# RG-LRU column order, taps read from PSUM, a fifth result place and three order changes in a fused decoder layer

## The chip, the cores and the metric

One core of a Trainium2 chip runs the whole step as one program. The metric is device microseconds of one execution. The engines are TensorE (PE, with its weight loads PEld), VectorE (DVE), ScalarE (ACT), GpSimd (POOL) and the queue engine SP, which only issues transfers.

## What is computed

One layer of a hybrid decoder, for a prompt of 2048 tokens and 8 sample tokens, with D = 1024. The input is normalized and modulated, and one projection `z = hn @ w_in` gives the columns `xa`, `za` (1024 each, for the RG-LRU group) and `q`, `k`, `v`, a low-rank decay and `zg` (for the GLA group). What matters here is the RG-LRU group:

```
xp = concat([conv0, xa], time)                      # 3 old rows in front
xc = conv_b + sum(xp[:, j:j+T] * conv_w[j] for j in range(4))
gx = sigmoid(blockdiag(xc) + b_gate_x);  ga = sigmoid(blockdiag(xc) + b_gate_a)
log_a = 8 * ga * log_sigmoid(lru_lambda);  a = exp(log_a)
h = scan(a, sqrt(1 - a*a) * gx * xc)                # h[t] = a[t] h[t-1] + ...
y_lru = h * silu(za)
```

The GLA group gives `y_gla = rmsnorm(o) * g * silu(zg)`, and both go through `w_out`, a gate, a residual add and a last RMSNorm. The prompt's outputs are compared beside the new states, among them the last three rows of `xa`.

## The kernel before, in words

The prompt is handled in two halves of 1024 tokens (`half` 0 and 1), each in two segments of 512 (`s` 0 and 1). Channels lie on the 128 partitions and tokens along the free axis. All matrix products are fp32 split into a rounded high part and a low rest, three matmuls for one.

The order on TensorE is: a start that loads, normalizes and begins the first GLA head (0 to about 90 us); the GLA heads of half 0 (to 332); the **couples** of half 0 (to 594); the GLA heads of half 1 (to 867); the couples of half 1 (to 1110); and the output projection (to the end).

**Couples** (class `Couple`, `couples()`). A couple is two blocks of 128 columns of the projection, computed for both segments by a Strassen-like scheme of seven products instead of eight. A product is 12 matmuls of 128x512. Products 0 and 3 build up bank `x`, products 2 and 5 bank `zz` (both from the four `acc` banks of PSUM), and 1, 4 and 6 bank `y` (of two `tp` banks). After product 3 the bank `x` holds segment 0 of the first column block; after product 4, line 1597 writes segment 1 of the second block into `x`; after product 5 `zz` holds segment 0 of the second block; after product 6 `y` holds segment 1 of the first. `block(s, n, src)` takes each result. The products of neighbouring couples are interleaved: m2, m3, (m+1)0, m4, m5, (m+1)1, m6, where m2 is product 2 of couple m. Line 1592 writes bank `zz` from `y` after product 2 and must have read `y` before product 4 adds to it.

Two kinds of couples exist. `Zg` holds two blocks of `zg`: each result goes through `silu` on ScalarE into a place `zs`, is multiplied on VectorE (line 1649) with a piece of `o` loaded from DRAM, and is stored. `Lru` holds a block of `xa` and one of `za`. A `za` result goes through `silu` into a place `zs` and waits for the scan. An `xa` result goes into `conv` (lines 1683 to 1706): ScalarE copies it to the tile `xa` behind 3 old columns (L1697) and computes the fourth tap (L1698); VectorE adds the three other taps from the tile `xa` (L1700, three of them), and the result is split into `xh` (ScalarE, L1705) and `xl` (VectorE, L1706). `gates(s)` multiplies `xh` and `xl` on TensorE with two gate matrices (six matmuls, L1718 to L1721) into the two banks `gps` (tags `kv` and `o`), which ScalarE empties by Tanh (L1722). After `gates(1)` come Exp, Sqrt and a Silu of one element named `one` (L1731 to L1733, with a table load each), two products (L1739, L1740) and the scan (L1746) on VectorE, and the results `zs` times the scan (L1757). The tiles `tx`, `tg` and `a` of the gates exist once, so the next couple's Tanh waits for the scan. There are four `zs` places.

**What sets the order.** `after(units, fn)` puts a step off; `tick(0.5)` follows each product, so a unit is two products. `behind(V)` keeps an instruction behind the last one recorded on VectorE. The order on each engine is then made by a planner from estimated durations, the earlier recorded instruction first among those that it holds ready. The first head and the output projection are `in_order`: their order is as written.

**First head** (`gla_head` with `wv`): `vhave(n)` splits the raw value weights of the second head into a high part (ScalarE, L379) and a low part (VectorE, L380), 1.5 and 2.5 units on.

**Output projection** (class `Pair`, lines 2183 and on): for two rows of tokens at once at first, seven products (B11, T2, T1, B21, T3, B22, T4) with weights loaded at its beginning; `split_w` makes their high (L2058) and low parts (L2061), `hi` and `lower` those of the operands S3 and S4, and `sums` (L2217) empties PSUM. `at(g, k, ...)` lists what follows product k of group g.

Of the kernel before, what the change touches and what calls it, by code (L numbers as in the profile page):

```python
# [8 lines left out]
F32 = mybir.dt.float32  # L9
# [44 lines left out]
def hybrid_kernel(ctx, tc, i, o):  # L54
# [1113 lines left out]
    def gla_head(half, h, k, wv=None, w=None):  # L1168
# [34 lines left out]
        if not final:  # L1203
            m = HEADS[k + 1]
            vcols = [(V0 + m * DV, DV, k0, 4) for k0 in (0, 4)]
            vraw = [None, None]

            def vrows(n):
                vraw[n] = ahead(*vcols[n])

            def vhave(n):
                w[n] = take(*vcols[n], vraw[n])

            if half == 0:
                for n in range(2):
                    after((0.5, 0.5)[n] if wv else (1, 1.5)[n], lambda n=n: vrows(n))
                    after((1.5, 2.5)[n] if wv else (2.5, 3.5)[n], lambda n=n: vhave(n))
            else:
                for n in range(2):
                    after((0.5, 2.5)[n], lambda n=n: vhave(n))  # L1220
# [261 lines left out]
    banks, turns = [0], [0, 0, 0, 1]  # L1482
# [5 lines left out]
    class Couple:  # L1488
# [115 lines left out]
        def zs(self):  # L1604
            own = self.more.pop(0) if self.more else None
            if own:
                return own()
            return lp.tile([P, 512], F32, tag="zs", name="zs", bufs=4)
# [3 lines left out]
    class Zg(Couple):  # L1612
# [26 lines left out]
        turn = 0  # L1639
# [5 lines left out]
        def block(self, s, dt, src):  # L1645
            z = self.zs()
            silu(z, src)
            c0 = SEGS[s][0]
            V.tensor_tensor(z, z, self.o[((0, 0), (1, 1), (0, 1), (1, 0)).index((s, dt))], op=OP.mult)
            late_spill(z, 8 + 2 * self.h + dt, self.half, c0)  # L1650
# [3 lines left out]
    class Lru(Couple):  # L1654

        def __init__(self, half, j):
            super().__init__(half, (XA + j * P, ZA + j * P), (16 + j, 8 + j))
# [16 lines left out]
        def block(self, s, n, src):  # L1674
            if n == 1:
                z = self.zs()
                silu(z, src)
                after(2, lambda: self.out(s, z))
            else:
                self.conv(s, src)  # L1680
                after((3.5, 2)[s], lambda: self.gates(s))

        def conv(self, s, src):
            j = self.j
            if s == 0:
                self.cv, self.x2 = [None] * 2, [None] * 2
                self.xa = lp.tile([P, 512 + 4], F32, tag="xa", name="xa")
                if self.half == 0:
                    V.memset(self.xa[:, :3], 0.0)
                else:  # L1690
                    V.tensor_copy(self.xa[:, :3], xac[:, j])
            else:
                V.tensor_copy(self.xa[:, :3], self.xa[:, 512:515])
            xa = self.xa
            cv = self.cv[s] = lp.tile([P, 512], F32, tag=f"cv{s}", name="cv")
            cw = [vecT[:, j, R_CW + k:R_CW + k + 1] for k in range(4)]
            S.copy(xa[:, 3:515], src)  # L1697
            S.activation(cv, src, AF.Identity, scale=cw[3], bias=vecT[:, j, R_CB:R_CB + 1])  # L1698
            for k in range(3):
                V.scalar_tensor_tensor(cv, xa[:, k:k + 512], cw[k], cv, op0=OP.mult, op1=OP.add)  # L1700
            if s == 1:
                V.tensor_copy(xac[:, j] if self.half == 0 else stT[:, j, 0:3], xa[:, 512:515])
# [217 lines left out]
    for k, h in enumerate(HEADS):  # L1920
        w = gla_head(0, h, k, wv0 if k == 0 else None, w)
        if k == 0:
# [10 lines left out]
    zg0.more = [None] * 2 + [lambda: lp.tile([P, 512], F32, tag="cv1", name="zs"),  # L1933
                             lambda: lp.tile([P, 512 + 4], F32, tag="xa", name="zs")[:, :512]]
# [512 lines left out]
    at(0, 1, later(first_two, first_s3), later(first_two, hi, S3), later(first_two, lower, S3), later(load_w, 0, B22, 5))  # L2447
    at(0, 2, later(split_w, 0, T3), later(first_two, first_s4_end), later(load_w, 0, T4, 6))
    at(0, 3, later(first_two, hi, S4), later(split_w, 0, B22), later(first_two, lower, S4), pairs[2].load)
# [98 lines left out]
```

## Time and profile before

| | |
|---|---|
| median of 3 runs | 1442.52 us (1440.55 to 1443.47) |
| profiled execution | 1444.88 us, of which the span from first to last instruction is 1443.1 us |
| mean granted clock of TensorE | 0.993 of full speed |
| busy share of the span | PE 98%, PEld 81%, DVE 74%, ACT 50%, POOL 15% |
| moved by DMA | 341.88 MB, mean 237 GB/s |

In the profile, a line such as L1718 is a line of the kernel before. Times are microseconds from the first instruction. A row of the timeline gives start, duration, engine, line, operation, tiles, shape and count, and in brackets how long the engine was idle before it and what ended that. Matmuls overlap, so their starts tell more than their durations.

### The profile page before, as it was taken

The page shows a single profiled execution, that of the slowest core. Times are in us where ns is not written, and L with a number is a line of the kernel's source. Part 1 is how long each engine was busy: PE and PEld are TensorE (multiplying, and loading weights), DVE is VectorE, ACT ScalarE, POOL GpSimd, SP SyncE. Part 2 cuts the span into 40 slices and gives each one's busy share as a digit, 9 for nine tenths or more (in the row PEclk, how much of TensorE's full clock was granted, in tenths as well). Part 3 has the DMA queues.
Part 4 walks back from the last instruction along what each step waited for, and adds up shares of the span by engine and source line. Part 5 has one row for each costly group of instructions (what it writes and reads, how often), then busy time and mean ns, then how long its engine had stood idle before and what let it go on. Part 6 is the DMA issues. An engine that isn't in the chain of part 4 may idle for free.

```text
span 1443.1 us, 22452 instructions
## 1 busy us (share of the span) xinstructions
PE 1408.6 (98%) x8113; PEld 1166.8 (81%) x8113; DVE 1062.9 (74%) x2335; ACT 725.4 (50%) x1354; POOL 215.6 (15%) x267
## 2 busy tenths in 40 slices
PE   8999999999999999999999999999999999999997
PEld 6888989886877777889898888877888787777886
DVE  5767985657879786766787864787854986597886
ACT  3634454635785878434353433767663622244432
POOL 0200153325232223101112100000012000000000
PEclk9999999999999999999999999999999999999999
DMA  9724755738688476965956529898879777684442
GB/s 320 279 82 158 263 202 199 243 132 288 244 284 297 171 240 238 385 212 172 321 193 233 197 88 319 281 313 282 279 241 407 287 262 237 246 322 149 148 162 102
DMA packets 168899, 341.88 MB, mean 237 GB/s; under 512 B 12466, under 2 KB 96722, under 8 KB 165197
## 3 DMA queue, kind: packets, MB, share of 16 engines
q1 hardware_dynamic: 136981, 275.82, 55.7%
q0 software_dynamic: 14480, 51.26, 9.2%
q10 hardware_dynamic: 17328, 13.37, 2.8%
q8 instruction: 64, 1.05, 0.3%
q14 instruction: 46, 0.38, 0.1%
HBM read 205.78 MB, written 134.69 MB: 236 GB/s over the span
## 4 chain that ended last, share of the span: by engine, by line
PE 61%; DVE 16%; ACT 11%; DMA 6%; issue 4%; POOL 2%; SPq 0%; ACTq 0%; DVEq 0%; POOLq 0%
PE acc L2196 11%; PE tp L2196 8%; PE acc L1582 5%; PE tp L1582 5%; PE acc L707 3%; PE acc L709 3%; PE acc L708 3%; PE acc L402 3%; PE acc L401 3%; PE acc L403 3%; DVE cv L1700 2%; PE po L1070 2%; DVE a L1746 2%; DVE op L1529 2%; DMA wr<-in_w_in_dram 1%
## 5 line engine op out<-in xcount | busy, mean ns | idle before, releaser
L1582 PE MATMUL acc<-op,op 128*128 128x512 f32 x1056 | 252.2, 391 | 0.0
L1582 PEld LDWEIGHTS acc<-op,op 128*128 128x128 f32 x1056 | 197.1, 188 | 42.1 <-issue 0.8
L1582 PE MATMUL tp<-op,op 128*128 128x512 f32 x792 | 192.2, 395 | 3.2 <-DVE acc L1592 2.4
L2196 PE MATMUL acc<-w,a 128*128 128x512 f32 (+1 forms) x792 | 187.5, 389 | 1.5 <-DVE a L2061 1.3
L1582 PEld LDWEIGHTS tp<-op,op 128*128 128x128 f32 x792 | 148.1, 189 | 39.7 <-issue 3.3
L2196 PEld LDWEIGHTS acc<-w,a 128*128 128x128 f32 x792 | 146.5, 188 | 37.8 <-issue 3.4
L401 PE MATMUL acc<-w,op 128*128 128x256 f32 (+1 forms) x508 | 150.7, 297 | 1.3 <-ACT w L379 1.2
L403 PE MATMUL acc<-w,op 128*128 128x256 f32 (+1 forms) x508 | 144.8, 285 | 0.3 <-DVE op L271 0.2
L402 PE MATMUL acc<-w,op 128*128 128x256 f32 (+1 forms) x508 | 144.7, 285 | 0.4 <-DVE w L380 0.4
L2196 PE MATMUL tp<-w,a 128*128 128x512 f32 x564 | 137.5, 393 | 1.2 <-DVE w L2061 1.2
L2196 PEld LDWEIGHTS tp<-w,a 128*128 128x128 f32 x564 | 105.1, 188 | 29.5 <-issue 5.2
L707 PE MATMUL acc<-op,w 128*128 128x512 f32 x296 | 121.1, 409 | 0.0
L709 PE MATMUL acc<-op,w 128*128 128x512 f32 x296 | 116.5, 394 | 0.0
L708 PE MATMUL acc<-op,w 128*128 128x512 f32 x296 | 115.9, 392 | 0.0
L401 PEld LDWEIGHTS acc<-w,op 128*128 128x128 f32 x508 | 96.9, 191 | 2.9 <-ACT w L379 1.6
L402 PEld LDWEIGHTS acc<-w,op 128*128 128x128 f32 x508 | 96.3, 190 | 1.6 <-DVE w L380 0.6
L403 PEld LDWEIGHTS acc<-w,op 128*128 128x128 f32 x508 | 96.3, 190 | 1.1 <-DVE op L271 0.4
L2058 ACT CAST a<-s 128x512 fp32r<-128x512 f32 x61 | 36.5, 620 | 106.4 <-issue 35.4
L228 ACT ACTIVATE junk<-on 128x256 bf16<-128x256 f32 x64 | 26.8, 418 | 120.1 <-DVE on L1075 103.1
L1700 DVE SCALAR_TENSOR_TENSOR cv<-xa,vecT,cv 128x512 f32<-128x512 f32 x96 | 77.0, 802 | 5.1 <-ACT cv L1698 4.2
L717 POOL DMA_DIRECT2D mixd<-zs x37 | 27.8, 754 | 282.7 <-DVE zs L1757 225.6
L1071 DVE TENSOR_TENSOR states<-states,pkv 128x256 f32<-128x256 f32 x60 | 25.0, 417 | 60.8 <-PE po L1070 60.5
(444 smaller groups left out, 2836.8 us busy)
## 6 DMA issues: line engine op xcount, KB each, us to landing
wtd<-op SPq DMA_DIRECT2D x77, 512.0 KB
op<-wtd SPq DMA_DIRECT2D x77, 512.0 KB
w<-parts SPq DMA_DIRECT2D x16, 1024.0 KB
a<-mixd SPq DMA_DIRECT2D x63, 256.0 KB
parts<-w POOLq DMA_DIRECT2D x12, 1024.0 KB, 6.6
w<-wd SPq DMA_DIRECT2D x10, 1024.0 KB
mixd<-zs POOLq DMA_DIRECT2D x37, 256.0 KB, 6.1
wr<-in_w_in_dram SPq DMA_DIRECT2D x18, 512.0 KB
```

The source lines that it names most:

```text
L401: PE.matmul(ps, part(0, kt, c), hi[:, kt % 4], start=kt == 0, stop=False)
L402: PE.matmul(ps, part(0, kt, c), lo[:, kt % 4], start=False, stop=False)
L403: PE.matmul(ps, part(1, kt, c), hi[:, kt % 4], start=False, stop=kt == KT - 1)
L707: PE.matmul(ps[:, :n], hi[:, kt], a, start=kt == 0, stop=False)
L708: PE.matmul(ps[:, :n], hi[:, kt], b, start=False, stop=False)
L709: PE.matmul(ps[:, :n], lo[:, kt], a, start=False, stop=kt == KT - 1)
L1070: PE.matmul(po, qi[:, t], St[h], start=False, stop=True)
L1529: V.tensor_tensor(w[:, 1], x, w[:, 0].bitcast(F32), op=OP.subtract)
L1582: PE.matmul(ps, w[:, u, k], t[:, v, k], start=q < 3 and (k, u, v) == (0, 0, 0), stop=(k, u) == (3, 1), skip_group_check=True)
L1700: V.scalar_tensor_tensor(cv, xa[:, k:k + 512], cw[k], cv, op0=OP.mult, op1=OP.add)
L2058: S.copy(t[:, 0, k], (low(t) if src is None else src)[:, k])
L2196: PE.matmul(ps, t[:, u, k], w[:, v, k, c], start=(q < 3 or ps is own) and (k, u, v) == (0, 0, 0), stop=(k, u) == (3, 1), skip_group_check= ...
```

## The change

The two column blocks of an `Lru` couple change places: `za` is the first and `xa` the second. So `za` comes out after products 3 and 6 and `xa` after 4 (segment 1, kept in its bank) and 5 (segment 0). Both segments' convolutions are recorded after product 5, `gates(0)` 2.5 units and `gates(1)` 3 units later. The tile `xa` and its copy are gone: the taps read the bank itself, shifted by the output's offset, and up to three columns at the left edge get small taps from the saved last three columns. The old tile's place serves as a fifth `zs`, each fifth time. `zg0`, the couple before the last of half 0, loses one extra place, and its third and fourth products with `o` are put off by 1.75 units and recorded `behind(V)`. In the first head the two `vhave` steps come 0.5 units earlier. In the output projection the splits of T3 and B22 each move one step ahead.

```diff
-                    after((1.5, 2.5)[n] if wv else (2.5, 3.5)[n], lambda n=n: vhave(n))
+                    after((1, 2)[n] if wv else (2.5, 3.5)[n], lambda n=n: vhave(n))
...
+            ring[0] += 1
+            if ring[0] % 5 == 0:
+                return lp.tile([P, 512 + 4], F32, tag="xa", name="zs")[:, :512]
             return lp.tile([P, 512], F32, tag="zs", name="zs", bufs=4)
...
+            def late():
+                with behind(V):
+                    mult()
+            if self.wait_o and s != dt:
+                after(self.wait_o, late)
+            else:
+                mult()
...
-            super().__init__(half, (XA + j * P, ZA + j * P), (16 + j, 8 + j))
+            super().__init__(half, (ZA + j * P, XA + j * P), (8 + j, 16 + j))
...
         def block(self, s, n, src):
-            if n == 1:
+            if n == 0:
                 z = self.zs()
                 silu(z, src)
                 after(2, lambda: self.out(s, z))
+            elif s == 1:
+                self.second = src
             else:
-                self.conv(s, src)
-                after((3.5, 2)[s], lambda: self.gates(s))
+                self.cv, self.x2 = [None] * 2, [None] * 2
+                self.conv(0, src)
+                self.conv(1, self.second)
+                after(2.5, lambda: self.gates(0))
+                after(3, lambda: self.gates(1))
...
-            if s == 0:
-                self.cv, self.x2 = [None] * 2, [None] * 2
-                self.xa = lp.tile([P, 512 + 4], F32, tag="xa", name="xa")
-                if self.half == 0:
-                    V.memset(self.xa[:, :3], 0.0)
-                else:
-                    V.tensor_copy(self.xa[:, :3], xac[:, j])
-            else:
-                V.tensor_copy(self.xa[:, :3], self.xa[:, 512:515])
-            xa = self.xa
...
-            S.copy(xa[:, 3:515], src)
             S.activation(cv, src, AF.Identity, scale=cw[3], bias=vecT[:, j, R_CB:R_CB + 1])
             for k in range(3):
-                V.scalar_tensor_tensor(cv, xa[:, k:k + 512], cw[k], cv, op0=OP.mult, op1=OP.add)
-            if s == 1:
-                V.tensor_copy(xac[:, j] if self.half == 0 else stT[:, j, 0:3], xa[:, 512:515])
+                n = 3 - k
+                V.scalar_tensor_tensor(cv[:, n:], src[:, :512 - n], cw[k], cv[:, n:], op0=OP.mult, op1=OP.add)
+                if s or self.half:
+                    V.scalar_tensor_tensor(cv[:, :n], xac[:, j, k:], cw[k], cv[:, :n], op0=OP.mult, op1=OP.add)
+            V.tensor_copy(stT[:, j, 0:3] if s and self.half else xac[:, j], src[:, 509:512])
...
-    zg0.more = [None] * 2 + [lambda: lp.tile([P, 512], F32, tag="cv1", name="zs"),
-                             lambda: lp.tile([P, 512 + 4], F32, tag="xa", name="zs")[:, :512]]
+    zg0.more = [None] * 2 + [lambda: lp.tile([P, 512], F32, tag="cv1", name="zs")]
+    zg0.wait_o = 1.75
...
-    at(0, 1, later(first_two, first_s3), later(first_two, hi, S3), later(first_two, lower, S3), later(load_w, 0, B22, 5))
-    at(0, 2, later(split_w, 0, T3), later(first_two, first_s4_end), later(load_w, 0, T4, 6))
-    at(0, 3, later(first_two, hi, S4), later(split_w, 0, B22), later(first_two, lower, S4), pairs[2].load)
+    at(0, 1, later(first_two, first_s3), later(first_two, hi, S3), later(first_two, lower, S3), later(split_w, 0, T3),
+       later(load_w, 0, B22, 5))
+    at(0, 2, later(first_two, first_s4_end), later(split_w, 0, B22), later(load_w, 0, T4, 6))
+    at(0, 3, later(first_two, hi, S4), later(first_two, lower, S4), pairs[2].load)
```

## Rows read from the trace of the kernel before

**Rows 1.** The page's busy time, share of the span and instructions of each engine

```profile
PE 1408.6 (98%) x8113; PEld 1166.8 (81%) x8113; DVE 1062.9 (74%) x2335; ACT 725.4 (50%) x1354; POOL 215.6 (15%) x267
```

**Rows 2.** TensorE's waits by line: released by, total us, times, longest us

```profile
PE gps L1718 <- ACT xh L1705: 4.4, 5, 1.5
PE tp L1582 <- DVE acc L1592: 2.4, 1, 2.4
...
PE pkv L1064 <- DVE kTl L1046: 1.7, 1, 1.7
...
PE acc L2196 <- DVE a L2061: 1.3, 1, 1.3
PE acc L401 <- ACT w L379: 1.2, 1, 1.2
PE tp L2196 <- DVE w L2061: 1.2, 1, 1.2
```

**Rows 3.** Stretches: length, busy time by engine, then granted clock, DMA share, GB/s

```profile
459.08:482.70 23.62, 23.62 (x117) 18.82 (x116) 17.06 (x22) 20.26 (x31) 5.83 (x4) 1.00 0.54 216
529.95:555.02 25.07, 24.27 (x117) 18.58 (x116) 21.41 (x30) 19.86 (x32) 6.79 (x5) 1.00 0.72 242
583.65:587.06 3.41, 3.33 (x8) 2.66 (x9) 3.38 (x5) 0.00 (x0) 0.01 (x1) 0.50 1.03 359
```

**Rows 4.** Timeline of TensorE from gates(0) to gates(1) of an early couple

```profile
367.30 0.62 PE L1721 MATMUL gps<-xl,amh 128*128 128x512 f32 x2
367.76 5.61 PE L1582 MATMUL acc<-op,op 128*128 128x512 f32 x24
373.21 0.40 PE L1718 MATMUL gps<-xh,amh 128*128 128x512 f32 x1
```

**Rows 5.** Timeline of PE, ACT and DVE around the seventh Lru couple of half 0

```profile
526.73 0.51 PE L311 MATMUL gps<-sel,am 128*128 128x8 f32 x4
...
526.94 0.20 ACT L1733 ACTIVATE one<-a 128x1 f32<-128x1 f32 x1
...
531.08 2.28 DVE L1746 TENSOR_TENSOR_SCAN a<-tg,tx 128x1024 f32<-128x1024 f32 x1
...
537.22 0.62 ACT L1705 CAST xh<-cv 128x512 fp32r<-128x512 f32 x1 [0.42 <-DVE cv L1700]
...
552.14 0.20 ACT L1733 ACTIVATE one<-a 128x1 f32<-128x1 f32 x1
```

**Rows 6.** VectorE's groups by line and shape: count, busy us, mean ns, idle before

```profile
L1700 DVE SCALAR_TENSOR_TENSOR cv<-xa,vecT,cv 128x512 f32<-128x512 f32 x96 | 77.0, 802 | 5.1 <-ACT cv L1698 4.2
...
L1289 DVE SCALAR_TENSOR_TENSOR xb<-acc,xb 128x512 f32<-128x512 f32 x7 | 4.8, 689 | 3.9 <-PE acc L709 3.9
...
L1702 DVE COPY xac<-xa 128x3 f32<-128x3 f32 x8 | 1.3, 163 | 1.6 <-ACT xa L1697 1.6
```

**Rows 7.** Timeline: last matmul of gates(0), and the Tanh emptying its second bank

```profile
370.04 0.68 ACT L1722 ACTIVATE tg<-gps,hba 128x512 f32<-128x512 f32 x1
...
530.99 0.63 PE L1721 MATMUL gps<-xl,amh 128*128 128x512 f32 x2
...
536.12 0.69 ACT L1722 ACTIVATE tg<-gps,hba 128x512 f32<-128x512 f32 x1 [1.98 <-DVE cv L1700]
```

**Rows 8.** Timeline of VectorE at the end of half 0's couples

```profile
577.70 1.22 DVE L1739 SCALAR_TENSOR_TENSOR a<-tg,a 128x1024 f32<-128x1024 f32 x1 [3.81 <-ACT one L1733]
...
582.98 0.69 DVE L1592 TENSOR_TENSOR acc<-tp,p 128x512 f32<-128x512 f32 x1
```

**Rows 9.** Timeline of ScalarE at the end of the first head

```profile
84.88 0.64 ACT L972 ACTIVATE e<-e 128x512 f32<-128x512 f32 x1
...
90.74 1.98 ACT L379 CAST w<-wr 128x1024 fp32r<-128x1024 f32 x2
```

**Rows 10.** Timeline of VectorE early in the output projection

```profile
1138.06 2.50 DVE L2061 TENSOR_TENSOR w<-w 128x512 fp32r<-128x512 f32 x4 [0.61 <-ACT w L2058]
1140.48 1.29 DVE L2061 TENSOR_TENSOR a<-s,a 128x512 fp32r<-128x512 f32 x2
```

More of the change, by code (lines that the diff above doesn't have):

```diff
@@ L1480, in open_s @@
         lp.tile([P, 1], F32, tag="one", name="place")
-    banks, turns = [0], [0, 0, 0, 1]
+    banks, turns, ring = [0], [0, 0, 0, 1], [0]
     def gps():
@@ L1637, in product @@
             super().product(q)
-        turn = 0
+        turn = wait_o = 0
         def load_o(self, n):
@@ L1648, in block, with mult @@
             c0 = SEGS[s][0]
-            V.tensor_tensor(z, z, self.o[((0, 0), (1, 1), (0, 1), (1, 0)).index((s, dt))], op=OP.mult)
-            late_spill(z, 8 + 2 * self.h + dt, self.half, c0)
+            x = self.o[((0, 0), (1, 1), (0, 1), (1, 0)).index((s, dt))]
+            def mult():
+                V.tensor_tensor(z, z, x, op=OP.mult)
+                late_spill(z, 8 + 2 * self.h + dt, self.half, c0)
+            def late():
[5 more added lines that the diff above has]
+                mult()
     smp_lru = {}
```

## The prediction, as written before the result was known

> **What bounds the kernel now.** I read the busy times first: TensorE is busy for 1408.6 us of a span of 1443.1, and the next engine, VectorE, for 1062.9 [rows 1]. The change takes no matmul away, so what it can win is TensorE's 34.5 us of idle time and what that idle time costs in clock. The second view is therefore TensorE's list of waits [rows 2]. Six of its rows are places that the change touches or lies beside: 4.4 us before `gates` (five times, released by the cast `xh`), 2.4 us once before a product of a couple (released by L1592 on VectorE), 1.7 us in a GLA chunk, 1.3 and 1.2 us early in the output projection, 1.2 us at the first product of the second head. The third view is the clock in stretches [rows 3]: in 583.65 to 587.06, which begins as the 2.4 us wait ends, the granted clock is 0.50, that is the level of 1.2 GHz instead of 2.4. TensorE was full before that wait. So this wait cost 2.4 us and half of 3.41 us more, 1.7, together 4.1.
>
> Next, why `xh` is late. An undisturbed couple takes 23.62 us and has no idle TensorE; the seventh `Lru` couple of half 0 takes 25.07, with 24.27 busy [rows 3]. Around it, `one` runs at 526.94 and again at 552.14 [rows 5]: ScalarE and VectorE need 25.2 us for a round that TensorE does in 23.6. The round is visible: `one` ends the chain of table loads, VectorE may then run L1739 and so on to the scan at 531.08, the taps of segment 1 come among and behind these, `xh` ends at 537.84, then come the gates, their Tanh, and the next chain to `one`. Product 6 ended just before the small matmuls at 526.73 [rows 5], so this convolution took 11.1 us, where TensorE has only three products and one set of gates to do in between. A product is 2.72 us (5.45 for two, from start to start) and a gate matmul 0.23, six of them 1.4 [rows 4]: 9.6 us with what is left of the small matmuls some 10.0. It does not fit, and the gates wait.
>
> **The convolutions and gates.** `xa` now leaves the couple after products 4 and 5, and both convolutions are recorded after product 5. From there to `gates(1)` TensorE has five products, one set of gates and in half 0 the small sample matmuls: 5 x 2.72 + 1.4 = 15.0 us, and 16.4 in half 0 (a 23.62 us couple has 1.8 beyond seven products, 19.0, and two sets of gates, 2.8; I take 1.4 of it for the sample matmuls, an estimate). In that time there must now be two convolutions. The worst old one, 11.1 us, plus three more taps of 0.69, three small ones of 0.16 (the three-column copy, the nearest row) makes 13.7 [rows 5, 6]. The margin is 2.7 us in half 0 where it was below zero. In half 1, by the same sum with the longest wait of 1.5 [rows 2] added to 9.6 and 2.6 to 3.1 more for two convolutions, 14.2 stands against 15.0: little, but not late. `gates(0)` come a product and their own 1.4 us ahead of that, 12.3 us behind product 5 in half 0, with one convolution to wait for. I take 4.0 of the 4.4 us as won; the ends are 0 (convolutions start later than recorded, since ScalarE is in its table chain) and 4.4.
>
> The round itself also gets shorter, by this sum: after `one`, L1739 and L1740 (1.2 each, L1739 in [rows 8]), six taps with their small ones (about 5), `xh` 0.6, gates 1.4, then Tanh and the chain as before, about 8.5: some 18 to 19 us. The path over the scan (2.3 behind the taps, then the next Tanh, which writes the tiles that the scan reads) comes to 21 or 22. Both are below 23.6, so lateness should not grow from couple to couple. These are estimates from the rows' durations; the order is the planner's.
>
> What the edit does to the engines: ScalarE loses 32 copies, VectorE loses 48 tiny instructions and gets 32 copies and 72 small taps (three at each `conv` but the first segment of half 0): 56 more at 0.16, 9 us. The taps themselves go from 802 ns with both inputs in SBUF to the 689 ns of the same operation with one input in a bank [rows 6]: 96 x 0.113 = 10.8 us less. So VectorE's load stays as it is; all of it lies beside TensorE. Bound: if a tap from a bank is no faster, 9 us more over 16 couples, 0.6 each, out of a margin of 2.7.
>
> The Trainium skill speaks against this edit: VectorE: DVE Perf Modes, section Rules for kernel authors, says to copy out of PSUM first if many operations follow, and its section on the TRN2 errata gives an instruction that reads PSUM 62 cycles of 0.96 GHz more, 65 ns. By it the taps would take 6.2 us more instead of 10.8 less, 0.4 us per couple's six, an estimate from that page; the row of L1289 against that of L1700 says the opposite.
>
> Banks: bank `x` now stays taken until the taps of segment 1 are done. Of the four `acc` banks three are in use when (m+2)0 takes one, so it is not what TensorE waits for. The silu of product 3 must be done before L1597 overwrites `x`; it is recorded ahead of the gates' Tanh and has two products' time. The fifth `zs` place covers the result that now comes earlier and lives longer: without it a fifth would be needed at product 3. I cost these at nothing; if the cover fails, a silu waits for a store, and a couple is late by a microsecond or two.
>
> **The end of half 0.** The 2.4 us wait is for L1592 at 582.98, on a VectorE that had stood idle for 3.81 us until `one` let L1739 start at 577.70 [rows 8]; three products with `o` and two splits then stood ahead. The change moves two of those (0.6 each) behind L1592, and with the gates no longer late `one` comes at least 1.6 us earlier (the two waits of half 0, 0.8 each, inside the 4.4). 1.2 + 1.6 is more than 2.4. What is put off has only its store, on POOL's queue, behind it, and no product of TensorE. I take all of it, 4.1 with the clock; ends 0 and 4.1.
>
> **The first head.** The split L379 ran at 90.74 behind the Exps of the decay; recorded one step earlier it can follow L972, which ends at 85.52 [rows 9]. The low part is 1.2 us of VectorE put into a chain that then delivers everything else 1.2 later, and the second half's low part may become the late one. The store of the split weights, which POOL issues half a unit behind, comes earlier with it, on a queue with nothing else to do there. Of the 1.2 us [rows 2] I take 0.8; ends -0.6 and 1.2.
>
> **The output projection.** T3's low parts come before two `sums`, so its wait (1.2) goes. But the next one, for the low part of S4 at 1140.48 [rows 10], stands behind the same VectorE work in another order: it can come earlier only by the idle 0.61 at 1138.06, which came from ScalarE doing S4 before B22. TensorE gets there earlier and waits longer. Net 0.6 of 2.5; ends 0 and 2.5. SP's order does not change; ScalarE asks for B22's weights about 4 us earlier, and if they have not landed by then the split waits for them, which is the end at 0.
>
> **Sum.** 4.0 + 4.1 + 0.8 + 0.6 = 9.5 us. The profiled execution took 1444.88 us, 1.78 more than its span, and lies 2.4 above the median of 1442.52. It would come to 1435.4, the median to 1433.0.
>
> **The rivals.**
> *A new wait on the `gps` banks (slower).* Between `gates(0)` and `gates(1)` there is now one product, 2.72 us, instead of two, and both need the same two banks. In the seventh couple the last matmul of `gates(0)` ended at 531.62 and the second bank was empty at 536.81, 5.2 us later [rows 7], 2.0 beyond a product and the two matmuls (0.47) before that bank is needed; in the early couple it was 367.92 to 370.72, 2.8, covered [rows 4, 7]. The taps now queue ahead of the scan for which the Tanh waits, which makes it worse. 16 couples at half of 2.0 up to all of it lose 16 to 32 us; at 17, 1442.5 - 9.5 + 17 = 1450. It decides from 0.6 us a couple. Against it: the order is free on TensorE, so the next product can go ahead, and `gates(0)` come 2.72 us later themselves, by which most of the 5.2 has passed. Chance 0.15.
> *The convolutions start no earlier.* ScalarE is in its table chain when product 5 ends, and the fourth tap comes behind `one`; the gates wait as before. Then 5.5 us remain: 1437. For it: `one` at 526.94 is about when product 6 ended. Chance 0.18.
> *Nothing in sum.* The planner makes a new order everywhere behind the first edit, and waits of 1 to 2 us, some with 1.7 us of slow clock, come up elsewhere: 1440 to 1445. Chance 0.12.
>
> **Chances and range.** Forecast 1433, its own range 1428 to 1437, 0.55. Below lie cases where the 1.7 us in the GLA chunk [rows 2] happens to go too. Two parts in a thousand, 2.9 us, is what a measurement here tells from no change: faster than 1439.6 is the forecast and most of the second rival, 0.71; same 0.14; slower 0.15. The range for 8 in 10 is 1427 to 1444.
>
> **What would show it.** TensorE's wait for `xh` gone from its list, couples 23.6 us apart through half 0, no clock of 0.50 near 580, L1700 near 0.69. T3's wait gone and the S4 wait near 1.8. Wrong: rows in which PE waits at L1718 for ACT's Tanh, or a new wait above 1.5 us with a drop of the clock behind it.

## The result: slower by 0.85 %, and the profile after

The changed kernel takes 1455.22 us (median of 6 runs, 1453.47 to 1457.58) against 1442.08 (6 runs, 1440.55 to 1444.74): a ratio of 1.0085, 95 % interval 1.0071 to 1.0098. The forecast was 1433.0, the range ended at 1444. Its profiled execution took 1455.03 us with a span of 1453.2, 10.1 more than the span before. The busy times of the page, then TensorE's list of waits (released by, total us, times, longest us):

```profile
PE 1412.1 (97%) x8113; PEld 1166.2 (80%) x8113; DVE 1059.4 (73%) x2391; ACT 709.2 (49%) x1322; POOL 219.8 (15%) x267
```

```profile
PE acc L401 <- DMA w<-parts: 3.8, 1, 3.8
PE gps L311 <- ACT am L305: 3.6, 4, 1.1
PE gps L1729 <- ACT xh L1716: 3.3, 2, 2.4
PE gps L1729 <- ACT tx L1733: 2.7, 7, 0.7
PE gps L304 <- DMA raw<-in_w_in_dram: 2.2, 3, 0.8
...
PE tp L2207 <- DMA w<-wd: 1.9, 1, 1.9
PE acc L2207 <- DVE a L2072: 1.8, 1, 1.8
```

Beside [rows 2]: the waits for `xh` (L1716, before L1705) are fewer but not gone, the wait of 2.4 us for L1592 shrank to two of 0.3, and the two of 1.2 us are gone. New are the waits for Tanh (`tx`) and for two loads of weights (`parts`, `wd`); those for `am` and for the load `raw` were 0.4 and 0.3 us before. In the couples of half 0 TensorE waits for `am` (3.6), `raw` (2.2) and Tanh (1.2) and no longer for `xh`; in those of half 1 for `xh` (3.3) and Tanh (1.4). Behind the waits for `parts` and `wd` the clock fell, which the stretches show (length, busy times, then granted clock, DMA share, GB/s):

```profile
597.03:600.44 3.41, 3.41 (x17) 3.41 (x16) 1.63 (x2) 2.48 (x3) 1.06 (x2) 0.50 1.02 420
1126.10:1129.51 3.41, 3.41 (x10) 2.64 (x9) 1.46 (x3) 0.62 (x1) 0.00 (x0) 0.50 1.04 412
```

Each begins 0.8 and 1.0 us after TensorE's wait (3.84 and 1.86 us) had ended, and in it the granted clock is 0.50, that is 1.2 GHz. With half of 3.41 us the first of them costs 5.5 us, the second 3.6.

The lengths of the stages in us, from TensorE's timeline. The first ends at the second head's first product. The couples are counted from the start of their first matmul to the start of their last one, so the wait of 3.84 us for half 1's first weights, and the slow clock behind it, stand in the row of the GLA heads of half 1. "RG-LRU alone" is an experiment below.

| stage | before | after | RG-LRU alone |
|---|---|---|---|
| start | 91.8 | 89.6 | 91.5 |
| GLA heads, half 0 | 240.7 | 238.9 | 237.6 |
| couples, half 0 | 260.9 | 263.5 | 263.5 |
| GLA heads, half 1 | 273.9 | 278.4 | 276.9 |
| couples, half 1 | 242.1 | 246.8 | 245.8 |
| output projection and end | 333.8 | 336.0 | 336.6 |

The couples of half 0 lost most of the wait at the end of the stage (4.1 us expected there) and still got 2.6 longer, those of half 1 4.7. What happened in them is to be seen on ScalarE. Its timeline in the kernel before has the fourth tap (L1698), the first of the chain of three table loads, the copy `am`, and segment 1's copy and fourth tap:

```profile
513.70 0.78 ACT L1698 ACTIVATE cv<-acc,vecT 128x512 f32<-128x512 f32 x1
...
520.47 1.28 ACT L1731 ACT_TABLE_LOAD   x1
...
525.28 0.35 ACT L305 COPY am<-gps 128x256 f32<-128x256 f32 x1
...
529.03 0.60 ACT L1697 COPY xa<-tp 128x512 f32<-128x512 f32 x1
529.51 0.80 ACT L1698 ACTIVATE cv<-tp,vecT 128x512 f32<-128x512 f32 x1
```

Segment 0's convolution began 6.8 us ahead of the chain of Exp, Sqrt and Silu, segment 1's behind it (`one` at 526.94, [rows 5]). The same place in the changed kernel: TensorE's product 5 (it ends at 518.60), VectorE's L1597, which puts product 4's result into its bank (until 520.13), then ScalarE:

```profile
515.72 2.88 PE L1582 MATMUL acc<-op,op 128*128 128x512 f32 x12
```

```profile
519.44 0.69 DVE L1597 TENSOR_TENSOR acc<-tp,p 128x512 f32<-128x512 f32 x1
```

```profile
518.47 1.28 ACT L1742 ACT_TABLE_LOAD   x1
519.77 1.24 ACT L1742 ACTIVATE tg<-tg,lc 128x1024 f32<-128x1024 f32 x1
521.01 1.28 ACT L1743 ACT_TABLE_LOAD   x1
522.31 1.06 ACT L1743 ACTIVATE a<-a 128x1024 f32<-128x1024 f32 x1
523.28 0.76 ACT L1707 ACTIVATE cv<-acc,vecT 128x512 f32<-128x512 f32 x1
524.05 1.28 ACT L1744 ACT_TABLE_LOAD   x1
525.35 0.20 ACT L1744 ACTIVATE one<-a 128x1 f32<-128x1 f32 x1
525.46 0.76 ACT L1707 ACTIVATE cv<-acc,vecT 128x512 f32<-128x512 f32 x1
...
526.63 0.37 ACT L305 COPY am<-gps 128x256 f32<-128x256 f32 x1
...
535.60 0.62 ACT L1716 CAST xh<-cv 128x512 fp32r<-128x512 f32 x1 [1.73 <-DVE cv L1712]
...
552.39 0.20 ACT L1744 ACTIVATE one<-a 128x1 f32<-128x1 f32 x1
```

Both convolutions now fall into the chain. They begin at 523.28, 4.7 us after product 5, and the last cast ends at 536.22. The copy `am`, for which TensorE waits at L311, ran between Sqrt and the last table load before (525.28); now the Identities stand there, and it comes behind them. From `one` to `one` it is 27.0 us, where it was 25.2 [rows 5]. VectorE in the same stretch:

```profile
524.07 1.53 DVE L1710 SCALAR_TENSOR_TENSOR cv<-acc,vecT,cv 128x509 f32<-128x509 f32 x2 [3.94 <-ACT cv L1707]
...
530.59 0.74 DVE L1710 SCALAR_TENSOR_TENSOR cv<-acc,vecT,cv 128x510 f32<-128x510 f32 x1
...
532.13 2.28 DVE L1757 TENSOR_TENSOR_SCAN a<-tg,tx 128x1024 f32<-128x1024 f32 x1
```

It idles 3.94 us for the first tap, and then taps stand ahead of the scan, which runs 6.8 us behind `one` (4.1 before [rows 5]). In most couples the scan is recorded at the end of the next couple's product 5, as before; new is that this couple's convolutions are recorded in that product, ahead of it. Over the whole kernel VectorE stood still for the Identity 39.2 us, where it was 4.2 [rows 6]; the row of its list of waits:

```profile
DVE cv L1710 <- ACT cv L1707: 39.2, 14, 5.1
```

In half 1 it goes further; in one round `one` and the scan are 14.2 us apart:

```profile
967.02 0.20 ACT L1744 ACTIVATE one<-a 128x1 f32<-128x1 f32 x1
```

```profile
981.17 2.34 DVE L1757 TENSOR_TENSOR_SCAN a<-tg,hc,tx 128x1024 f32<-128x1024 f32 x1
```

### The profile page after: what moved, and what is told of

Same layout as the page of the kernel before. It is cut to its first block, busy times and chain, and to the rows that moved or that the text cites. A ratio compares the mean times of both kernels' runs of the same rounds, so it can differ in the third digit from the quotient of the medians.

```text
span 1453.2 us, 22466 instructions
## 1 busy us (share of the span) xinstructions
PE 1412.1 (97%) x8113; PEld 1166.2 (80%) x8113; DVE 1059.4 (73%) x2391; ACT 709.2 (49%) x1322; POOL 219.8 (15%) x267
## 4 chain that ended last, share of the span: by engine, by line
PE 60%; DVE 17%; ACT 8%; DMA 7%; issue 5%; POOL 3%; SPq 1%; ACTq 0%; DVEq 0%; POOLq 0%
PE acc L2207 11%; PE tp L2207 8%; PE acc L1582 6%; PE tp L1582 4%; PE acc L401 4%; PE acc L402 4%; PE acc L403 4%; PE acc L707 3%; PE acc L709 3%; PE acc L708 3%; DVE cv L1710 3%; DVE a L1757 2%; PE po L1070 2%; DMA wtd<-op 1%; DVE op L1529 1%
## 5 line engine op out<-in xcount | busy, mean ns | idle before, releaser
L401 PE MATMUL acc<-w,op 128*128 128x256 f32 (+1 forms) x508 | 151.0, 297 | 3.9 <-DMA w<-parts 3.8
L401 PEld LDWEIGHTS acc<-w,op 128*128 128x128 f32 x508 | 97.1, 191 | 5.5 <-issue 4.2
L1710 DVE SCALAR_TENSOR_TENSOR cv<-acc,vecT,cv 128x510 f32<-128x510 f32 (+2 forms) x96 | 71.0, 742 | 40.0 <-ACT cv L1707 39.2
```

What stands on the lines that cost most here:

```text
L401: PE.matmul(ps, part(0, kt, c), hi[:, kt % 4], start=kt == 0, stop=False)
L1710: V.scalar_tensor_tensor(cv[:, n:], src[:, :512 - n], cw[k], cv[:, n:], op0=OP.mult, op1=OP.add)
```

## The experiments

All were timed in turns with the kernel before; the number in brackets is the 95 % interval of the ratio, and runs of different experiments are best compared by these ratios. Several expectations count in products what the edit gives in units of `after`. A unit is two products, and the product in which a step is put off already counts as its first half unit. So the three experiments on the time of the gates move them by one product; "half a product later" moves the convolutions to the end of product 5, ahead of the next product; and the first segment's convolution that is put off by one unit is recorded one product later, ahead of product 4, and not "with the sixth product".

**The parts alone.** The kernel before with one part of the change: the RG-LRU part (columns, convolutions, gates, bank taps, fifth place), the late multiplications of `zg`, the first head's earlier `vhave`, the output projection's order. Then the last three together. Edits as in the diff above.

> The kernel before with the RG-LRU part alone (columns exchanged, both convolutions recorded with the sixth product, taps from the projection's banks, fifth place). Theory T (the two convolutions together make ScalarE's and VectorE's round longer than TensorE's 23.6 us, and the lateness is passed on to the DMA queue that starts half 1 and the output projection): the whole loss is here, 1456 to 1461 us, the stages of couples 2 to 5 us longer each, VectorE's scan 4.6 us or more behind ScalarE's Silu load. Rival A (the couples lose only what their own stages show, the rest of the loss comes from the gate columns' late multiplications and the small order changes): 1446 to 1450 us. Rival B (the convolutions are harmless): 1438 to 1442 us.

> The kernel before with the gate columns' late multiplication (1.75 products) alone. Theory T: the 2.4 us stall at 582.98 and the dip of the clock at 583.65 go and nothing takes their place, 1437 to 1439 us. Rival A: half 1's first weights come late as in the changed kernel (3.8 us at 596.2 and a dip of the clock there), 1441 to 1446 us.

> The kernel before with the first head's value rows half a product earlier alone. Theory T: 0.8 us less, 1440.5 to 1442 us. Rival (it also takes away the stall near 225 us and its dip of the clock, which the changed kernel no longer has): 1438.5 to 1440 us.

> The kernel before with the output projection's new order alone. Theory T: 0.6 us less, 1441 to 1442 us; the changed kernel's 2.5 us longer output projection comes from the couples being late, not from this order. Rival A: the new order itself costs there, 1443 to 1445 us.

> The kernel before with the three small parts (first head, late multiplications of the gate columns, output projection) and without the RG-LRU part. All theories: the three ratios measured alone (0.9992, 0.9995, 0.9993) multiply to 0.998, 1439 to 1441 us. If a transfer that sets the start of half 1 or of the output projection takes over: 1442 us.

RG-LRU alone: 1454.2, 1.0070 [1.0047, 1.0093]. `zg` alone: 0.9992 [0.9979, 1.0006]; first head: 0.9995 [0.9982, 1.0009]; output projection: 0.9993 [0.9982, 1.0004]; the three together 0.9992 [0.9978, 1.0005]. So nearly the whole loss is in the RG-LRU part (2 us below theory T's range, the stages longer as T said), and the other three win nothing that can be measured, alone or together. With `zg` alone TensorE's waits show where part of its 4 us went:

```profile
PE acc L898 <- DMA wr<-in_w_in_dram: 1.6, 2, 1.0
...
PE tp L1582 <- DVE acc L1592: 1.2, 1, 1.2
...
PE acc L401 <- DMA w<-parts: 0.9, 1, 0.9
```

The wait for L1592 fell from 2.4 to 1.2; then TensorE came earlier to half 1's first weights and waited for them, and for `wr`.

**Scan ahead of the taps, first try.** The first tap of each convolution pinned behind the last recorded scan.

```diff
+                with tc.issue_after(tail[0]) if tail[0] is not None and k == 0 else ExitStack():
+                    V.scalar_tensor_tensor(cv[:, n:], src[:, :512 - n], cw[k], cv[:, n:], ...)
```

> The changed kernel, but VectorE's first tap of each convolution is pinned behind the scan of the block before, so that the scan runs first again. Theory T (the taps that stand ahead of the scan make the round long): the scan comes again about 4 us behind the small Silu instead of up to 14, the waits on Tanh (1.6 and 2.5 us) and most of the late stores and loads go, 1448 to 1452 us. Rival B (what hurts is that both convolutions now come late and together; putting the scan ahead only makes the casts xh later, and the gates wait for them instead): 1455 to 1462 us, Tanh waits exchanged for longer waits on xh.

1453.0, 1.0068 [1.0053, 1.0083]. It changed nothing: in all rounds but one the scan still ran 4.6 to 13.5 us behind `one`, because a block's scan is recorded after the next block's convolutions, so the pin caught the scan of one block earlier. It decides nothing about T.

**Convolutions recorded at the end of product 5**, and so behind the scan of the couple before, in both halves, and then in half 0 alone.

```diff
-                self.conv(0, src)
-                self.conv(1, self.second)
+                def convs():
+                    self.conv(0, src)
+                    self.conv(1, self.second)
+                after(0.5, convs)
```

> The changed kernel, with both convolutions recorded half a product later, behind the copy of the sampled columns' sums. Rival C (ScalarE's order: the two Identity instructions of the convolutions stand ahead of the copy am, and TensorE waits for that copy, 4.3 us in the couples of half 0): those waits fall to the 0.6 us of before, 1450 to 1453 us. Theory T: the copy comes earlier, but the casts xh come later by as much, 1454 to 1458 us.

> The changed kernel with both convolutions recorded half a unit (one product) later in half 0 alone, where that gave couples of 259 us against 263.5, and as changed in half 1. Theory B with the lateness passed on to half 1's first weights: couples of half 0 at 259 us and the stall on these weights under 1 us instead of 3.8, with its dip of the clock gone: 1446 to 1449 us. Rival (the first weights of half 1 are late by themselves): 1450 to 1453 us.

Both halves: 1459.9, 1.0115 [1.0098, 1.0132]; rival C's waits went, its time didn't come, and it is 2 us above T's range too. The scan is back at 3.8 us behind `one` in most rounds of half 0, the waits for `am` are nearly gone and half 0's couples take 259.2 us; but half 1's take 259.3 against 246.8, and the gates wait for `xh`:

```profile
PE gps L1731 <- ACT xh L1718: 12.3, 9, 2.5
```

Half 0 alone: 1450.5, 1.0059 [1.0045, 1.0072], couples of half 0 at 259.6: the rival's range. The couples came out as expected, the stall on half 1's weights did not: still 2.7 us. So in half 0 the taps ahead of the scan do cost some 4 us (for T), and putting them behind it costs more in half 1 (for B).

**Second segment earlier.** Identity and wide taps of segment 1 recorded with product 4.

```diff
             elif s == 1:
                 self.second = src
+                self.taps(1, src)
```

> The changed kernel, but the second segment's Identity and its three wide taps are recorded with the fifth product, where that segment arrives; only its three narrow taps wait for the first segment. Rival B (both convolutions at once are the cause): most of the waits on xh, am and Tanh go, 1446 to 1450 us. Theory T (taps ahead of the scan): there are as many of them ahead of the scan, the scan is no earlier, 1453 to 1457 us.

1464.5, 1.0138 [1.0122, 1.0154]: against both theories. ScalarE's timeline says why recording earlier didn't mean running earlier:

```profile
527.03 1.06 ACT L1750 ACTIVATE a<-a 128x1024 f32<-128x1024 f32 x1
528.00 0.76 ACT L1708 ACTIVATE cv<-acc,vecT 128x512 f32<-128x512 f32 x1
528.78 1.28 ACT L1751 ACT_TABLE_LOAD   x1
```

The result of product 4 also falls into the chain: L1597 has it in its bank at 524.88, the chain runs from 523.20 to 530.27. So its convolution still starts between Sqrt and Silu. And the small taps and `xac` now hold up the bank: 2.5 us of new waits of products for `xac`.

**Gates wider apart**: `after(2.5, ...gates(0))` to `after(2, ...)`. This gives `gates(0)` the place among the products that they had in the kernel before.

> The changed kernel with the first segment's gates 2 products behind the convolutions instead of 2.5, so that the two sets of gates are a whole product apart, not half. Rival D (gates too close together, so that the second set waits for the banks until Tanh has read them: 1.6 and 2.5 us): these waits go, 1450 to 1452 us. Theories T and B: TensorE then waits for xh instead, 1454 to 1459 us.

1462.9, 1.0137 [1.0120, 1.0153]. Rival D falls: Tanh waits are left (1.6 us in four, 2.7 before this edit), and `xh` costs up to 5.6 us at once. That `gates(0)` come a product later in the changed kernel is not what made it slow.

**Scan ahead of the taps, second try.** The scan recorded with the second gates, and the taps pinned behind it.

```diff
-            after(0.5, self.scan)
+            self.scan()
```

> The changed kernel with the scan recorded together with the second gates (a product before the next block's convolutions, where it was recorded after them) and the first tap of each convolution pinned behind it: VectorE now has scan, output products, then taps. Theory T (taps ahead of the scan are the cause): the scan comes some 4 us behind the small Silu everywhere, 1447 to 1451 us. Rival B (from the sixth product on there is too little time for both convolutions beside the scan: whichever of the two is second is late): the Tanh waits go, the waits of the gates on xh grow as they did when the convolutions were recorded a step later (4.5 and 9.6 us), 1455 to 1462 us.

1492.8, 1.0337 [1.0308, 1.0365]. Now the scan does run 3.1 to 3.7 us behind `one` in nearly every round, and the kernel is 36 us slower than the changed one by the two ratios. T falls as the main cause: with the scan first the kernel is far slower. VectorE stands still at the head of its queue until `one` is there (first row, of its own list of waits), and what TensorE needs of it comes late (second row, TensorE's list):

```profile
DVE a L1752 <- ACT one L1746: 53.1, 15, 8.1
```

```profile
PE tp L1582 <- DVE acc L1592: 17.3, 9, 4.8
```

**Taps from SBUF in the changed kernel**: the old body of `conv` with the copy to `xa`; columns, time and gates as changed. The tile `xa` takes its place back, so the fifth `zs` place is gone as well.

```diff
-                V.scalar_tensor_tensor(cv[:, n:], src[:, :512 - n], cw[k], cv[:, n:], ...)
+                V.scalar_tensor_tensor(cv, xa[:, k:k + 512], cw[k], cv, ...)
```

> The changed kernel, but with the tile xa and its copy again: the taps read SBUF as before, and columns, times and order are the changed ones. Rival E (taps from the bank are the cause: they hold the banks): 1444 to 1449 us. Theories T and B (the bank is harmless, the time of the convolutions is the cause): as slow as the changed kernel or slower by the two copies of 0.57 us in each round, 1455 to 1462 us.

1468.6, 1.0158 [1.0122, 1.0194], some 10 us slower than the changed kernel by the ratios, and above the ranges of all three theories. E gets no support, and in the changed kernel's list no product waits for a tap. What the copies cost and what the lost fifth place costs, this run doesn't tell apart.

**Only the second segment from the bank**, columns and times as before, with the three small parts; then the same in half 1 alone.

```diff
+            if s:
+                self.bank_taps(src)
+                return
```

> The kernel before with the three small parts, and in the RG-LRU columns only the second segment's taps read from the projection's bank (that segment's copy and the shift of three columns go; columns, times and the first segment stay as before). Theory B: the convolutions stay apart, each round saves a copy of 0.57 us on ScalarE, and VectorE's taps get 0.06 us shorter: the waits of the gates on xh fall, 1437 to 1440 us. Rival E (taps from a bank hold it and TensorE waits for the bank): 1443 to 1450 us, with new waits of the products on a bank.

> The kernel before with the three small parts, and in half 1 alone the second segment's taps from the projection's bank (in half 0 that kernel's couples took 261.9 us against 257.1, in half 1 240.4 against 241.5). Theory B: 1439 to 1441 us, the first version that would beat both. Rival (differences of a microsecond in the couples are taken back by the transfers that follow): 1441 to 1443 us, no different from the kernel before.

In both halves 1445.5, 1.0005 [0.9994, 1.0016]: neither B's gain (the waits for `xh` stay at 4.2 us) nor E's waits for a bank. In half 0 one wait of 2.4 us for `am` came up. In half 1 alone 1439.5, 0.9983 [0.9973, 0.9992].

**First segment's convolution put off by one unit in the kernel before**, from a copy made after product 3. It is recorded after the next couple's product 0, ahead of product 4.

```diff
             S.copy(self.xa[:, 3:515], src)
+            if s == 0:
+                after(1, lambda: self.taps(0, self.xa[:, 3:515]))
+            else:
+                self.taps(1, src)
```

> The kernel before, in which only the first segment's convolution is put off: its block is still copied to xa after the fourth product, but its Identity, taps and casts are recorded two products later, with the sixth product, as in the changed kernel. Columns, gates, banks and the second segment's convolution stay. Theory B (the convolution of the first segment was worth its place two products earlier; put beside the second one it makes ScalarE's and VectorE's round late): slower, 1452 to 1468 us, with waits on am, Tanh or xh as in the changed kernel and rounds of 26 us or more from one small Silu to the next. Rival F (it is the exchange of the columns, through z and the order of the output products, not the time of the convolution): 1441 to 1446 us, waits as before.

1438.7, 0.9969 [0.9957, 0.9981]: faster, and outside both ranges. It does not decide on B, since the convolution is not beside the second one, as B's price supposes. The rows of ScalarE:

```profile
510.82 0.57 ACT L1694 COPY xa<-acc 128x512 f32<-128x512 f32 x1
...
513.08 0.82 ACT L1704 ACTIVATE cv<-xa,vecT 128x512 f32<-128x512 f32 x1
...
516.91 1.28 ACT L1737 ACT_TABLE_LOAD   x1
```

Put off, it still starts ahead of the table chain, by 3.8 us, from data that lies ready in SBUF. TensorE's waits for `xh` fell with it to 1.1 us in the whole kernel, in two, where they were 4.4 [rows 2]; both are in half 1.

**The recorded time of the gates.** Second gates (and what hangs on them) a product earlier in the changed kernel, a product later in the kernel before.

```diff
-                after(3, lambda: self.gates(1))
+                after(2.5, lambda: self.gates(1))
```

```diff
-                after((3.5, 2)[s], lambda: self.gates(s))
+                after((3.5, 2.5)[s], lambda: self.gates(s))
```

> The changed kernel with the second gates recorded one product (0.5 unit) earlier, together with the first ones, as in the kernel before; what hangs on them (Exp, Sqrt, scan) is recorded a product earlier too, so that the scan stands again before the next block's convolutions. Theory G (the product by which the second gates and the scan were put off is the cause): 1440 to 1448 us, the scan 4 us behind the small Silu. Theory H (the blocks of xa come later: segment 0's with the sixth product instead of the fourth, so that its convolution and casts cannot be done by the time of the gates): still 1452 to 1464 us, with the waits of the gates on xh grown.

> The kernel before with the second gates, and so Exp, Sqrt and scan, recorded one product (0.5 unit) later, nothing else. Theory G: 1450 to 1460 us, the scan 4.6 us or more behind the small Silu and Tanh waits. Theory H: 1440 to 1446 us.

Earlier in the changed kernel: 1478.8, 1.0262 [1.0241, 1.0284], although the scan is back at 3.3 to 3.8 us in most rounds. TensorE then waits for Tanh and `xh`:

```profile
PE gps L1729 <- ACT tx L1733: 10.1, 7, 2.0
PE gps L1729 <- ACT xh L1716: 8.9, 3, 6.1
```

Later in the kernel before: 1446.6, 1.0031 [1.0019, 1.0044], with the scan 3.0 to 4.9 us behind `one`, not later than before, against G. So second gates a product later cost about 4 us there. G falls by the first run; H has the sign of both, but the first is 15 us beyond its range and the second 0.6 us. G also supposes a difference that the two kernels don't have: `gates(1)` are recorded after product 0 of the couple after the next in both (2 units from product 6 before, 3 units from product 5 now), and the scan with them. These two runs tell what it costs to move the second gates, not what the change moved.

**The gains together**: the three small parts, the first convolution put off, and in half 1 segment 1 from the bank.

> The kernel before with what gained or at least did not lose so far: the first segment's convolution put off by two products from a copy that is made at once (0.997 alone), the three small parts, and in half 1 the second segment's taps from the bank (0.998 together). Theory H (what the convolutions need is time between the arrival of their data and the gates; here the first has 15 us and its data is there from the fourth product, the second as before): no new waits, 1434 to 1438 us, faster than both kernels. Rival: both gains are the same waits on xh in half 1, taken away twice, 1438 to 1440 us, no better than the better of the two.

1439.7, 0.9982 [0.9971, 0.9993]: faster than both kernels, but not better than the first convolution put off alone: the rival's range, not H's. The couples of half 0 fell to 255.8 us, the shortest of all, and half 1's weights took it back, with a stretch of slow clock that began in this wait and went on behind it (589.50 to 593.00 at 0.50):

```profile
PE acc L401 <- DMA w<-parts: 3.9, 1, 3.9
```

## Why the prediction was wrong, step by step

**The step that failed** is the sum of the convolutions: 13.7 us of work, set against the time from the end of product 5 to `gates(1)` ("The margin is 2.7 us in half 0", and 14.2 against 15.0 in half 1). It lets both convolutions start when the product ends. In the couple shown ScalarE had gone into its table chain at 518.47, product 5 ended at 518.60, and product 4's result was in its bank at 520.13. The first Identity came at 523.28, 4.7 us after product 5, and the last cast ended at 536.22, 17.6 us after it instead of 13.7 and past the 16.4 that were counted. From the first Identity on it took 12.9 us. (The 13.7 already hold one late start: the old convolution of 11.1 us, from which they were made, began at 529.03, 2.3 us after product 6.)

What this cost is not what the sum looked at. In half 0 no gates waited for `xh` any more, where it had been 0.8 us twice. TensorE had been held up by other things first:

```profile
519.34 1.07 PE L304 MATMUL gps<-raw,fs 128*32 128x256 f32 x16 [0.74 <-DMA raw<-in_w_in_dram]
...
527.05 0.61 PE L311 MATMUL gps<-sel,am 128*128 128x8 f32 x4 [0.96 <-ACT am L305]
...
538.03 0.50 PE L1729 MATMUL gps<-xh,amh 128*128 128x512 f32 x1 [0.67 <-ACT tx L1733]
```

In half 1, where the margin was 0.8, two waits for `xh` are left, 0.95 and 2.38 us, where three had made 2.8. So of the 4.4 us only 1.1 were won, and the waits that the prediction put at nothing grew by 7.8: `am` from 0.4 to 3.6, Tanh from none to 2.7, `raw` from 0.3 to 2.2. For `am` the rows show the reason, the Identities ahead of it on ScalarE. The load `raw` was asked for at 512.36, where it had been 506.07; what held it back is not shown.

The prediction had the late start as a rival (chance 0.18, "ScalarE is in its table chain when product 5 ends, and the fourth tap comes behind `one`") and gave it 1437, as if it only forfeited the 4.0 us. That price was the second error. The kernel before had one convolution ahead of the chain and one behind it; the changed one has both in it.

How far this is shown: that nearly the whole loss lies in the RG-LRU part is measured (1.0070 of 1.0085). That both convolutions begin inside the chain, and what TensorE then waits for, are rows. That the start inside the chain is the cause is argued. Seven runs kept the exchanged columns and moved a step or the scan; the best is 1.0059, and none got both convolutions ahead of the chain in most couples. Nearest to a test come the two that record the convolutions at the end of product 5: in half 0 they then begin behind `one` and let `am` and the scan go first, and the couples there are 4.3 and 3.9 us shorter than in the changed kernel. So in half 0 the cost is in what the convolutions push back. In half 1 the same step cost 12.5 us, with the gates waiting for `xh`. In the changed kernel itself no gates waited in the four couples whose convolutions both began ahead of a chain (the first Identities at 352.85, 448.68, 887.82 and 987.66); they waited in eight of the other twelve. That is a coincidence in one trace, not a test. No run exchanged the columns and nothing else, and what the exchange costs by itself stays open.

**"The round itself also gets shorter"** (18 to 19 us, 21 or 22 over the scan): wrong. Between neighbouring `Lru` couples it was 27.0 us at its longest in half 0, and in half 1 up to 29.5. The sum added the durations of one chain and left out that the taps of two segments, the scan, the splits and the products' additions share VectorE in one order.

**The gates' 4.0 us**: the list has 3.3 us for `xh` left, 2.7 for Tanh new. The rival on the `gps` banks foresaw the Tanh waits and "the taps now queue ahead of the scan"; its price, 16 to 32 us, was about six times the 2.7 that this wait took, or more. That its 1450 lies nearest to the 1455 measured is luck. Wider gates did not help.

**The end of half 0, 4.1 us**: the wait for L1592 shrank to 0.6 in the changed kernel (and to half with `zg` alone), and the slow stretch was gone from there. But the 1.7 us for the clock are no fixed price: with the output projection's order alone the same wait of 2.4 us was there (it ended at 580.80), and the clock stayed at 1.00:

```profile
579.00:582.50 3.50, 1.70 (x7) 1.42 (x8) 3.50 (x4) 0.01 (x1) 1.24 (x2) 1.00 1.03 396
582.50:586.00 3.50, 3.50 (x17) 2.87 (x16) 2.80 (x6) 0.60 (x1) 1.50 (x2) 1.00 1.05 309
```

In the changed kernel the gain was given back at once: TensorE met half 1's first weights, 3.8 us and a slow stretch of 3.41. SyncE's queue shows that these were asked for hardly later than before (584.51 before):

```profile
574.32 1.72 SPq L1531 DMA_DIRECT2D wtd<-op  x2
...
584.99 2.10 SPq L348 DMA_DIRECT2D w<-parts  x2
```

The stores of the first row ran at 569.82 before, 4.5 us earlier, and all this lies in a stretch where the DMA share is 1.0, so more bytes stood in front. This is read from the rows, not tested. In the combined kernel they were asked for at 576.86 and TensorE waited 3.9 us all the same: what half 0's end wins, that transfer takes.

**First head and output projection, 0.8 and 0.6**: each mechanism came as said (the wait of L401 for L379 gone; T3's wait gone and S4's at 1.8, both in the list above), and neither moved the time by what a measurement tells: 0.9995 and 0.9993.

**The taps**: "802 ns to 689" failed in both numbers. The rows of before and after with shortest, median and longest duration:

```profile
L1700 DVE SCALAR_TENSOR_TENSOR cv<-xa,vecT,cv x96: 723/745/1778, 351.1 to 1060.7; 128x512 f32<-128x512 f32 x96
```

```profile
L1710 DVE SCALAR_TENSOR_TENSOR cv<-acc,vecT,cv x96: 719/742/750, 353.7 to 1068.7; 128x509 f32<-128x509 f32 x32, 128x510 f32<-128x510 f32 x32, 128x511 f32<-128x511 f32 x32
```

An ordinary tap takes the same from SBUF and from the bank. The mean of 802 [rows 6] held six taps of 1.6 to 1.8 us, and the bank taps have none. So the 65 ns more that the Trainium skill (VectorE: DVE Perf Modes, the TRN2 errata) led me to weigh do not appear, and neither does my saving per tap; what was saved was the long ones.

## What to carry to other kernels

Count a step's time from when its engine can begin it, not only from when its data is there: look where in the round the engine's blocking chain (here Exp, Sqrt and Silu with three table loads) stands, and whether a moved result arrives in front of it or inside it. A rival that "only forfeits the gain" should be priced by what then queues behind it on both engines. And before counting a gain at the end of a stage, look for the transfer that the next stage waits for: here three kernels that came to half 1 earlier waited 0.9 (`zg` alone), 2.7 (convolutions later in half 0) and 3.9 us (all gains together) for one.

## What the runs showed of the hardware

A tap with two SBUF inputs that begins while a GpSimd operation runs ends only after that operation; a bank tap doesn't wait for it. One of the long taps of the kernel before, and GpSimd at that time:

```profile
518.02 1.78 DVE L1700 SCALAR_TENSOR_TENSOR cv<-xa,vecT,cv 128x512 f32<-128x512 f32 x1
```

```profile
516.91 2.34 POOL L1550 TENSOR_TENSOR t<-raw,t 128x512 f32<-128x512 f32 x1 [2.00 <-DVE op L1529]
```

Of the 96 taps before, the 72 that overlapped no GpSimd instruction took 744 ns on average and 754 at most. Eleven overlapped only the issue of a transfer on GpSimd and took 739 to 749. Thirteen overlapped a GpSimd operation on tensors. The seven of them that began before it took 739 to 748; the six that began while it ran took 1583 to 1778, and each of these ended 0.55 us after it (here at 519.80, GpSimd at 519.25). Of the 96 bank taps seven began while such an operation ran; they took 721 to 749. The Trainium skill says that there is contention (GPSIMD Engine Reference, section Specifications: GpSimd's way to SBUF is shared with VectorE and contended by instructions with two SBUF inputs), and the rows agree. It is a reason to read one operand from a bank beside GpSimd work, if the bank's time allows it.
